# The first three loads of a streaming GELU-multiply kernel: from a critical section into the first block

## Chip, cores, metric

One core of a Trainium2 chip. The metric is the device time of one execution in microseconds (us). A profiled execution also has a span, from its first instruction to its last; the time is some 1.4 us longer than the span.

## The reference

```python
def setup_inputs():
    return {'x': np.random.randn(32, 512, 2048).astype(np.float32)}

def reference(x):
    half_dim = x.shape[-1] // 2
    x1, x2 = x[..., :half_dim].copy(), x[..., half_dim:].copy()
    gelu_x1 = 0.5 * x1 * (1 + erf(x1 / np.sqrt(2)))
    return (gelu_x1 * x2).astype(np.float32)
```

It reads 134.2 MB and writes 67.1 MB.

## The kernel before

The rows are cut into 16 tiles of 128 partitions x 8 rows. There are two input and two output buffers. SyncE issues the loads, ScalarE the GELU and most stores, VectorE the multiply, and the kernel owns all semaphores in the loop. A tile framework wraps only the beginning: it starts with an opening barrier and ends with a closing barrier (made by `tc.close()`), in each of which all engines wait for one another, and the first three loads are issued between the two. A semaphore is a counter that one instruction or transfer raises and another waits for; a load has landed when its semaphore says so.

```python
    def load(i, rows, sem):
        counted(
            nc.sync.dma_start(out=x_bufs[i % 2][:, rows, :], in_=x_t[i][:, rows, :]), sem, 16
        )
    ...
    with tc.tile_critical():
        load(0, slice(0, 4), first)
        load(0, slice(4, 8), loaded[0])
        load(1, slice(0, 8), loaded[1])
    tc.close()
    tc.compile()

    for i in range(n_tiles):
        k = i % 2
        last = i == n_tiles - 1
        pieces = i == 0 or last
        steps = ((0, 2), (2, 4), (4, 8)) if pieces else ((0, 5), (5, 8))
        if i >= 2:
            nc.scalar.wait_ge(stored[k], n[stored[k].name])
        for lo, hi in steps:
            rows = slice(lo, hi)
            if i == 0 and lo == 0:
                nc.scalar.wait_ge(first, n[first.name])
            elif lo == 0 or (i == 0 and lo == 4):
                nc.scalar.wait_ge(loaded[k], n[loaded[k].name])
            ...  # ScalarE: GELU of these rows; VectorE: multiply; in tile 0 a store, issued by ScalarE, behind rows 4 and 8
        ...      # other tiles: one store
        if i + 2 < n_tiles:
            nc.sync.wait_ge(mul_done, n[mul_done.name])
            load(i + 2, slice(0, R), loaded[k])
```

Of the kernel before, what the change touches and what calls it, by code (L numbers as in the profile page):

```python
# [1 line left out]

# [4 lines left out]

GELU = mybir.ActivationFunctionType.Gelu


@with_exitstack
def kernel(
    ctx: ExitStack,
    tc: tile.TileContext,
    x: bass.AP,
    out: bass.AP,
):
    nc = tc.nc
    P = nc.NUM_PARTITIONS

    x_flat = x.flatten_outer_dims()
    out_flat = out.flatten_outer_dims()
    n_rows, dim = x_flat.shape
    half = dim // 2

    R = 8
    x_t = x_flat.rearrange("(n p r) d -> n p r d", p=P, r=R)
    o_t = out_flat.rearrange("(n p r) d -> n p r d", p=P, r=R)
    n_tiles = x_t.shape[0]
    x_bufs = [nc.alloc_sbuf_tensor(f"x{k}_tile", [P, R, dim], x.dtype) for k in range(2)]  # L30
    o_bufs = [nc.alloc_sbuf_tensor(f"o{k}_tile", [P, R, half], out.dtype) for k in range(2)]

    first = nc.alloc_semaphore("first")
    loaded = [nc.alloc_semaphore(f"loaded{k}") for k in range(2)]
    stored = [nc.alloc_semaphore(f"stored{k}") for k in range(2)]
    gelu_done = nc.alloc_semaphore("gelu_done")
    mul_done = nc.alloc_semaphore("mul_done")
    tail_stored = nc.alloc_semaphore("tail_stored")
    n = {sem.name: 0 for sem in [first, *loaded, *stored, gelu_done, mul_done, tail_stored]}

    def counted(ins, sem, by):
        ins.then_inc(sem, by)
        n[sem.name] += by

    def load(i, rows, sem):
        counted(
            nc.sync.dma_start(out=x_bufs[i % 2][:, rows, :], in_=x_t[i][:, rows, :]), sem, 16  # L47
        )

    def store(queue, i, rows, sem):  # L50
        queue.wait_ge(mul_done, n[mul_done.name])
        counted(
            queue.dma_start(out=o_t[i][:, rows, :], in_=o_bufs[i % 2][:, rows, :]), sem, 16
        )



    with tc.tile_critical():  # L58
        load(0, slice(0, 4), first)
        load(0, slice(4, 8), loaded[0])  # L60
        load(1, slice(0, 8), loaded[1])
    tc.close()
    tc.compile()  # L63

# [14 lines that stand above are left out]
                nc.scalar.activation(  # L79
                    out=o_bufs[k][:, rows, :], in_=x_bufs[k][:, rows, :half], func=GELU  # L80
                ),
                gelu_done,
                1,
            )
            nc.vector.wait_ge(gelu_done, n[gelu_done.name])
            counted(
                nc.vector.tensor_mul(  # L87
                    out=o_bufs[k][:, rows, :],
                    in0=o_bufs[k][:, rows, :],
                    in1=x_bufs[k][:, rows, half:],  # L90
                ),
                mul_done,
                1,
            )
            if pieces and hi % 4 == 0:
                if last:
                    store(nc.sync, i, slice(hi - 4, hi), tail_stored)
                else:
                    store(nc.scalar, i, slice(hi - 4, hi), stored[k])
        if not pieces:  # L100
            if i == n_tiles - 2:
                store(nc.sync, i, slice(0, R), tail_stored)
            else:
                store(nc.scalar, i, slice(0, R), stored[k])
# [5 lines that stand above are left out]
    nc.scalar.drain()  # L110
    for sem in (first, *loaded, *stored):
        nc.scalar.sem_clear(sem)
    nc.vector.drain()
    nc.vector.sem_clear(gelu_done)
    nc.sync.sem_clear(mul_done)
    nc.sync.wait_ge(tail_stored, n[tail_stored.name]).then_inc(
        tail_stored, -n[tail_stored.name]
    )


# [1 line left out]
_INS = ['x']  # L122
_OUTS = [((32, 512, 1024), 'float32')]


# [23 lines left out]
```

## Time and profile before

| | before |
|---|---|
| time, median of the first 3 runs | 469.57 us (469.43 to 469.67) |
| span of the profiled run | 468.1 us |
| VectorE / ScalarE busy | 30% / 25% |
| DMA, mean over the span | 430 GB/s |
| first load issued / first packet / first activation | 0.94 / 1.95 / 12.99 us |

Read it from the ends inward. The compute engines are mostly idle and the DMA engines are busy throughout, so what counts is when the stream of 201.3 MB starts, whether it has holes, and its rate. The prediction shows the lines for each.

### The profile page before, as it was taken

What the parts mean: (1) busy time and instruction counts of PE and PEld (TensorE: products, weight loads), DVE (VectorE), ACT (ScalarE), POOL (GpSimd) and SP (SyncE); (2) the same over time, 40 slices, a digit from 0 to 9 for tenths busy, and PEclk for the clock granted to TensorE, in tenths of its full rate; (3) what the DMA queues carried; (4) which work ended last, traced back from release to release, by engine and by line L of the source; (5) the groups of instructions that cost most, each with busy time, mean ns of one, the idle gap of its engine ahead of it and who ended that gap; (6) DMA issues with size and microseconds to landing.
All of it is one profiled execution on the core that took longest, in us unless ns stands there. A gap on an engine that the chain in (4) does not pass through costs nothing.

```text
span 468.1 us, 174 instructions
## 1 busy us (share of the span) xinstructions
DVE 140.5 (30%) x34; ACT 115.5 (25%) x35; POOL 0.2 (0%) x4
## 2 busy tenths in 40 slices
DVE  0330514207052060511606116060150702507043
ACT  1320606032060410604106050050500506014060
POOL 0000000000000000000000000000000000000000
DMA  8999899999999999999999999999999999999998
GB/s 358 448 448 442 375 423 496 414 403 445 417 482 403 420 431 493 403 403 448 470 426 403 442 409 493 403 403 448 493 403 403 448 442 454 404 428 423 493 395 367
DMA packets 5041, 201.34 MB, mean 430 GB/s; under 512 B 560, under 2 KB 560, under 8 KB 560
## 3 DMA queue, kind: packets, MB, share of 16 engines
q1 hardware_dynamic: 2880, 142.61, 70.5%
q10 hardware_dynamic: 2160, 58.72, 29.1%
q14 instruction: 1, 0.01, 0.0%
HBM read 134.22 MB, written 67.11 MB: 430 GB/s over the span
## 4 chain that ended last, share of the span: by engine, by line
DMA 76%; DVE 14%; ACT 8%; ACTq 0%; SPq 0%; issue 0%
DMA out_dram<-o_tile 66%; DVE o_tile L87 14%; DMA x_tile<-in_x_dram 10%; ACT o_tile L79 8%; ACTq L110 0%; SPq L47 0%; SPq L63 0%; SPq L58 0%
## 5 line engine op out<-in xcount | busy, mean ns | idle before, releaser
L87 DVE TENSOR_TENSOR o_tile<-o_tile,x_tile 128x5120 f32<-128x5120 f32 (+3 forms) x34 | 140.5, 4170 | 320.2 <-ACT o_tile L79 320.2
L79 ACT ACTIVATE o_tile<-x_tile 128x5120 f32<-128x5120 f32 (+3 forms) x34 | 114.3, 3407 | 337.4 <-DMA out_dram<-o_tile 301.9
L79 ACT ACT_TABLE_LOAD x1 | 1.3, 1283 | 3.3 <-PEq L63 3.3
L133 POOL MEMSET const-bfloat16-1.0<- 128x1 bf16 x1 | 0.1, 102 | 0.0
L133 POOL MEMSET const-uint8-127<- 128x1 uint8 x1 | 0.1, 102 | 0.0
L133 POOL MEMSET const-float32-1.0<- 128x1 f32 x1 | 0.1, 99 | 0.0
L133 POOL MEMSET const-float32-0.0<- 128x1 f32 x1 | 0.1, 98 | 0.2 <-issue 0.2
## 6 DMA issues: line engine op xcount, KB each, us to landing
out_dram<-o_tile ACTq DMA_DIRECT2D x13, 4096.0 KB, 44.7
x_tile<-in_x_dram SPq DMA_DIRECT2D x2, 4096.0 KB, 16.7
out_dram<-o_tile ACTq DMA_DIRECT2D x2, 2048.0 KB, 34.4
out_dram<-o_tile SPq DMA_DIRECT2D x1, 4096.0 KB, 25.1
out_dram<-o_tile SPq DMA_DIRECT2D x2, 2048.0 KB, 7.6
x_tile<-in_x_dram SPq DMA_DIRECT2D x15, 44.5
```

Source lines behind the costliest of these rows:

```text
L79: nc.scalar.activation(out=o_bufs[k][:, rows, :], in_=x_bufs[k][:, rows, :half], func=GELU),
L87: nc.vector.tensor_mul(out=o_bufs[k][:, rows, :], in0=o_bufs[k][:, rows, :], in1=x_bufs[k][:, rows, half:],),
L133: nc = _bacc.Bacc("TRN2", target_bir_lowering=False, num_devices=1)
```

## The change

Intent: the critical section costs SyncE a nop and a branch ahead of the loads and some bookkeeping behind them. The new version issues the same loads as plain instructions of the framework's first block, and marks them so that the framework adds no semaphores of its own. The marking is needed: left out, the kernel does not build, as the framework then finds no room on these instructions for its own semaphore update.

```diff
     def load(i, rows, sem):
-        counted(
-            nc.sync.dma_start(out=x_bufs[i % 2][:, rows, :], in_=x_t[i][:, rows, :]), sem, 16
-        )
+        ins = nc.sync.dma_start(out=x_bufs[i % 2][:, rows, :], in_=x_t[i][:, rows, :])
+        counted(ins, sem, 16)
+        return ins
...
-    with tc.tile_critical():
-        load(0, slice(0, 4), first)
-        load(0, slice(4, 8), loaded[0])
-        load(1, slice(0, 8), loaded[1])
+    for ins in (
+        load(0, slice(0, 4), first),
+        load(0, slice(4, 8), loaded[0]),
+        load(1, slice(0, 8), loaded[1]),
+    ):
+        tc.no_tile_sem_insts.add(ins.ins.name)
     tc.close()
     tc.compile()
```

## The prediction

> **What bounds the kernel now.** I read the page first (spans, the 40 slices, the chain, the DMA queues), then the stretches table for the stages, then the chain in order of time, then the instructions of source lines L58, L47 and L63, because the change touches only the first 3.3 us.
>
> ```profile
> span 468.1 us, 174 instructions
> DVE 140.5 (30%) x34; ACT 115.5 (25%) x35; POOL 0.2 (0%) x4
> DMA  8999899999999999999999999999999999999998
> HBM read 134.22 MB, written 67.11 MB: 430 GB/s over the span
> ```
>
> Neither compute engine is busy a third of the span, while the DMA engines are in the top tenth in nearly every slice, the first and the last included. The stretches table gives the same by stage (columns: stretch, its length, busy time and instructions of VectorE, ScalarE and GpSimd, clock, DMA share, GB/s):
>
> ```profile
> 0.00:40.00 40.00, 8.92 (x3) 8.61 (x4) 0.20 (x4) 1.00 0.96 406
> ...
> 118.00:176.00 58.00, 17.52 (x4) 14.24 (x4) 0.00 (x0) 1.00 1.00 434
> ...
> 292.00:350.00 58.00, 17.52 (x4) 14.25 (x4) 0.00 (x0) 1.00 1.00 434
> ```
>
> The steady rate is 434 GB/s and two tiles (25.2 MB) take 58.0 us. The chain of waits puts 76% of the span on DMA; its other pieces (9 us of VectorE, 4.5 us of ScalarE) are latency while the DMA engines work on other tiles, as the full share of these stretches shows. So the kernel is a stream of 201.3 MB. A change can help only by starting the stream earlier, speeding it, or filling a hole in it. Before the stream there is this head of the chain:
>
> ```profile
> 0.67 0.05 issue
> 0.71 0.01 SPq L58
> 0.73 0.06 issue
> 0.78 0.03 SPq L63
> 0.82 0.12 issue
> 0.94 0.38 SPq L47
> ```
>
> L58 is the critical section, L47 the load. SyncE leaves the opening barrier at 0.67 us, runs a NOP of the critical section at 0.71, a compare-and-branch at 0.78 that leads into its block, and issues the first load only at 0.94. Finer stretches show when bytes move:
>
> ```profile
> 1.84:1.95 0.11, 0.00 (x0) 0.00 (x0) 0.00 (x0) 1.00 0.00 0
> 1.95:2.05 0.10, 0.00 (x0) 0.00 (x0) 0.00 (x0) 1.00 6.70 1966
> ...
> 466.00:467.00 1.00, 0.00 (x0) 0.00 (x0) 0.00 (x0) 1.00 0.99 426
> 467.00:468.00 1.00, 0.00 (x0) 0.00 (x0) 0.00 (x0) 1.00 0.05 16
> ```
>
> The first packets start at 1.95 us, 1.0 us after the first load's issue begins; the last end just after 467.0, and the final wait passes at 468.1. (A share over 1 appears because packets are booked at their start.) Hence: 0.94 us of prologue, 1.0 us of first latency, about 465.1 us of stream, 1.0 us of last latency. The reported 469.57 us is 1.4 us more than the span, a constant that I carry over.
>
> After the loads, the critical section and the closing of the block stand between SyncE and the barrier that frees the others:
>
> ```profile
> L58 SPq NOP  x2: 13/13/13, 0.7 to 2.5; - x2
> L58 SPq EVENT_SEMAPHORE  x1: 17/17/17, 2.3 to 2.3; - x1
> L58 SPq DRAIN  x1: 55/55/55, 2.4 to 2.4; - x1
> ```
>
> ScalarE waits behind that barrier until 3.28 us, loads its table for 1.28 us, and then waits again for the first load, which lands at 12.97:
>
> ```profile
> 3.28 1.28 ACT L79 ACT_TABLE_LOAD   x1 [3.28 <-PEq L63]
> 12.99 3.71 ACT L79 ACTIVATE o_tile<-x_tile 128x2048 f32<-128x2048 f32 x2 [8.43 <-DMA x_tile<-in_x_dram]
> ```
>
> It has 8.43 us of slack there.
>
> **What the Trainium skill says.** "DMA: Bandwidth & Descriptors", section "Where 436 GB/s comes from", gives 435.2 GB/s for the 16 ports; the trace agrees with 434 in the steady stretches, so the stream has nothing left to gain from a different start. The same page, "Latency and other measured facts", gives about 600 ns for the first byte of a hardware-generated DMA; the trace differs with 1.0 us from issue start to first packet, and I use 1.0. "Advanced Engine Details and Errata", "Control Flow Timing", gives about 108 ns for a compare-and-branch; the trace has 0.03 us recorded plus 0.12 us before the next instruction starts, 0.15 in all. "ScalarE: Activation LUTs", "What ACT_TABLE_LOAD costs", gives about 1283 ns; the trace agrees with 1.28 us.
>
> **The change part by part.** (1) *Removed ahead of the loads:* the entry NOP (0.71) and the branch with the gap behind it (to 0.94). If the loads stand in the first block, the first takes the NOP's place right after the opening barrier. 0.94 - 0.71 = 0.23 us, all on the path: the stream starts 0.23 us sooner, the first packets at about 1.72. (2) *Unchanged:* the three loads, their order, queue, sizes and semaphores. Their issue costs 0.94 to 2.27 = 1.33 us in total, and becomes 0.71 to about 2.04. Marking them as owned by the kernel only keeps the framework from adding its own semaphores and waits. (3) *Removed behind the loads:* the exit's semaphore event, drain and NOP, from 2.27 to 2.57 on SyncE, 0.3 us less perhaps 0.05 for the ordinary step to the next instruction, so about 0.25. With part 1 the closing barrier frees ScalarE about 0.23 + 0.25 = 0.48 us sooner, at about 2.8 instead of 3.28. That lies inside the 8.43 us of slack and is worth nothing. (4) *Moved:* the first activation waits for the first load, so it moves from 12.99 to about 12.76; from there each tile's work hangs on landings and on stores, and these shift by the same 0.23 us. Nothing in the loop changes, so no hole is filled and the rate stays 434 GB/s. Sum: -0.23 us on the path, +0; span 468.1 to about 467.9, time 469.57 to 469.34.
>
> **The rivals.** *A: the gain is swallowed.* The branch might stay ahead of the loads, or the first packets might wait on something that does not depend on the issue. For it: the first packets come 1.0 us after issue, longer than the page's 0.6. Against it: the branch carries a wait on the critical section's own semaphore and goes only to SyncE, so it belongs to the section. Time: 469.6. *B: the closing barrier now waits for the loads.* A section that hides its DMAs is gone, and a framework that waits at the block's end for every DMA in flight would hold ScalarE until all three loads land. They are 16.8 MB, at 434 GB/s some 38.7 us, so to about 40.5. Then come the barrier's rest (2.64 to 3.28, 0.64), the table (1.28), and ScalarE and VectorE from the first activation to the first store's issue (12.99 to 19.45, 6.46): the DMA engines would idle some 8.4 us plus the latency to the first byte, 1.0. Time: 469.3 + 9.4 = about 479, +2.0%. Against it: the point of marking the instructions is to leave them out of that bookkeeping. I give it 2 to 3%. *C: the framework's scheduler reorders the three loads*, for example the 8-row load ahead of tile 0's second half. The first store at 19.45 would stay; the second half would land only with the whole 16.8 MB plus the first store's 2.1 MB, near 45 us, and tile 0's reuse load and second store (issued at 30.80 now) would come only some 8 us of compute later (3.62 + 4.43), so again a hole of at most 8 us: about 477. Against it: all three are on one engine with no dependence among them; source order is the natural one. About 1%. *D: the new start disturbs the interleaving of loads and stores.* Both streams hang on the same events and move together, and the unchanged runs spread only 0.24 us; I allow 0.3 us either way.
>
> **Range and chances.** The centre is the main sum, rounded: 469.3. Rival A is 0.3 above; run-to-run spread is 0.24 us, and another chip or session can add a few tenths; 0.15% is 0.7 us. So 468.7 to 469.9. A gain of 2% (9.4 us) would need a hole in the stream that no stretch shows, or a rate above the 434 at which it already runs: 0.5%. A loss of over 2% needs B at the large end of its estimate: 1.5%. Within 2%: 98%.
>
> **What would show it right or wrong.** In the changed profile: no L58-like NOP or compare-and-branch ahead of the first load; its issue begins at 0.70 to 0.75; first packets at 1.7 to 1.75; the three issues still sum to about 1.33; the table load begins near 2.8; the first activation at about 12.76; loads and stores 0.2 us sooner everywhere; stretches of 58 us at 434 GB/s. Step 1 is wrong if the first issue stays near 0.94 (rival A) or if the first packets do not follow it. Rival B would show as a table load near 41 us, rival C as a second half of tile 0 landing after 40 us with the first activation still near 12.8, D as a later shift different from that of the first activation. My step 4 fails if the shift at the start is there, but the end comes no sooner.

## The result, and the profile after

| | before | after |
|---|---|---|
| time, median of 6 runs each | 469.59 us (469.43 to 469.67) | 469.38 us (469.27 to 469.52) |
| span of the profiled run | 468.1 us | 468.0 us |
| first load issued | 0.94 us | 0.73 us |
| first packet | 1.95 us | 1.74 us |
| table load of ScalarE | 3.28 us | 2.86 us |
| first activation | 12.99 us | 12.79 us |

The ratio is 0.9996, with a 95% interval of 0.9983 to 1.0009. The interval includes 1: these twelve runs alone do not show a gain, the experiments below pool more.

The chain of waits of the kernel after, in order of time (start, length, what), begins without the nop and the branch. SPq is an instruction in SyncE's queue, "issue" is time in which the engine waited for nothing that the profile shows; the load's line is now L46:

```profile
0.67 0.07 issue
0.73 0.38 SPq L46
1.11 0.05 issue
1.17 0.43 SPq L46
1.59 0.05 issue
1.64 45.50 DMA x_tile<-in_x_dram
```

SyncE leaves the opening barrier at 0.67 as before, and its next instruction is the load. Fine stretches of the kernel after (columns as in the prediction, the last is GB/s) show the bytes following by 1.0 us, the same steady rate, and an end that comes a few packets earlier (311 GB/s between 466 and 467 us, where the kernel before still had 426):

```profile
1.64:1.74 0.10, 0.00 (x0) 0.00 (x0) 0.00 (x0) 1.00 0.00 0
1.74:1.84 0.10, 0.00 (x0) 0.00 (x0) 0.00 (x0) 1.00 5.69 1638
118.00:176.00 58.00, 17.52 (x4) 14.24 (x4) 0.00 (x0) 1.00 1.00 434
466.00:467.00 1.00, 0.00 (x0) 0.00 (x0) 0.00 (x0) 1.00 0.73 311
```

The timeline of ScalarE in the kernel after (start, length, instruction, idle time before it and what ended it):

```profile
2.86 1.28 ACT L82 ACT_TABLE_LOAD   x1 [2.86 <-PEq L66]
12.79 3.71 ACT L82 ACTIVATE o_tile<-x_tile 128x2048 f32<-128x2048 f32 x2 [8.64 <-DMA x_tile<-in_x_dram]
```

The table load came 0.42 us earlier, and ScalarE only waits longer for the first load (8.64 us instead of 8.43). The activation moved by 0.20, as the load's issue did.

One thing in this pair of traces needed care: the shift is 0.20 us at the first activation, but 0.14 at the third tile-load's landing (47.28 against 47.14) and 0.11 at the end of the span. Was a part of the gain lost on the way, or is that noise?

### The profile page after: what moved, and what is told of

Same layout as the page of the kernel before. It is cut to its first block, busy times and chain, and to the rows that moved or that the text cites. A ratio compares the mean times of both kernels' runs of the same rounds, so it can differ in the third digit from the quotient of the medians.

```text
span 468.0 us, 167 instructions
## 1 busy us (share of the span) xinstructions
DVE 140.5 (30%) x34; ACT 115.5 (25%) x35; POOL 0.2 (0%) x4
## 4 chain that ended last, share of the span: by engine, by line
DMA 76%; DVE 14%; ACT 8%; ACTq 0%; SPq 0%; issue 0%
DMA out_dram<-o_tile 66%; DVE o_tile L90 14%; DMA x_tile<-in_x_dram 10%; ACT o_tile L82 8%; ACTq L113 0%; SPq L46 0%
```

## Experiments

The theory is that the time is the first load's issue plus a constant, the stream behind it. The main rivals: the earlier closing barrier makes the gain rather than the earlier loads; or the start is hidden and the 0.2 us are noise.

### The two kernels again

The first is the kernel before, unedited, the second the kernel after, unedited; so neither has a diff.

> The kernel before against itself, to learn how small a difference five rounds can show. Every theory: ratio 1.0000, medians within 0.1 us of each other, first load issued at 0.94 us, first activation at 12.99 us give or take 0.05, span 468.0 to 468.2 us. If the two medians differ by 0.2 us or more, the measured gain of the change (469.59 to 469.38) is not distinguishable from noise by times alone.

Measured: 469.56 us median of 5, against 469.54 for the other runs of the kernel before in those rounds; ratio 0.9998. The two means are 469.53 and 469.64, so even equal kernels differ by 0.1 us in one set of rounds: a single set cannot settle 0.2 us. The first load was issued at 0.94 us, the first activation came at 13.02, the span was 468.2.

> The changed kernel unedited, again. Main theory (the whole stream is moved forward by the earlier issue): 0.1 to 0.25 us faster than before, first load issued at 0.73 us, first activation near 12.79. In the first profile the shift against the kernel before was 0.20 us at the first issue and at the first activation but only 0.14 at the third landing and 0.10 at the last packet; if that loss is noise of the memory, this profile shows other values in the late stages with the same 0.20 at the start; if it is systematic, it shows the same decay. Rival A (gain swallowed): no difference in time.

Measured: 469.31 us median of 5 (469.22 to 469.60), ratio 0.9995 (0.9981 to 1.0008). The first load was again issued at 0.73. But the first activation came at 12.90 and the span was 468.2 us. So two profiles of the same kernel, with the same issue time, differ by 0.11 us at the first activation and by 0.2 us at the end. The "decay" of the shift in the first pair of traces is within that, and single profiles cannot resolve 0.2 us at the end of the span; the start of the loads, which repeats to 0.01 us, and many timed runs can. Over all runs the kernel before has a mean of 469.57 us (31 runs) and the kernel after one of 469.39 us (11 runs): 0.18 us, with a standard error that I put at 0.05 from the spread of some 0.13 us of single runs. The issue moved by 0.20 us. The kernel after ran beside the kernel before twice, and each time the means give much the same (0.18 us in the result, 0.21 us here).

### One part of the change at a time

An empty critical section put back behind the loads. The exit is back where it was; in the trace the section's own nop and branch come with it, but also behind the loads (2.10 and 2.17 us):

```diff
         tc.no_tile_sem_insts.add(ins.ins.name)
+    with tc.tile_critical():
+        nc.sync.nop(nofuse=True)
     tc.close()
```

> The changed kernel with an empty critical section behind the three loads: the exit instructions are back, the entry ones stay away from the loads. Main theory: first load issued at 0.73 us, ScalarE's table load starts later than the changed kernel's 2.86, at 3.1 to 3.4, and the time is that of the changed kernel (within 0.1 us), since ScalarE has over 8 us of slack there. Rival (the earlier closing barrier is what gains): the time goes back to that of the kernel before, +0.2 us.

Only the entry left: the kernel before, with the three instructions behind its loads taken out of the built program:

```diff
     tc.compile()
+    behind = next(b for b in nc.main_func.blocks if "_after_critical" in b.name)
+    behind.instructions = [
+        ins for ins in behind.instructions
+        if type(ins).__name__ not in ("InstNoOp", "InstDrain")
+    ]
```

> The kernel before with the three exit instructions of the critical section (nop, drain, nop) taken out; the loads still stand behind its entry nop and branch. Main theory: first load issued at 0.94 us, table load starts some 0.2 us earlier than 3.28, and the time is that of the kernel before (within 0.1 us). Rival (the exit is what cost the time): 0.2 us faster than before.

Measured: exit back, 469.37 us median of 5, first load at 0.73, table load at 3.26. Entry back, 469.45 us median of 5, first load at 0.94, table load at 3.13. The first is clear: a whole critical section behind the loads costs nothing measurable. The second lay between the two kernels, so I ran it again, together with a large dose of the other factor.

> The version with only the entry of the critical section left, again, as its first five runs (mean 469.46 us) lay between the two kernels: 0.07 us above the changed kernel and 0.11 below the kernel before. Main theory: the time of the kernel before, near 469.57 us, so that the mean of the ten runs is within 0.1 us of it. Rival: 469.4 again or less, and then the exit instructions have a share of some 0.1 us in the gain that the main theory does not explain.

Measured: 469.54 us median of 5 (469.53 to 469.60). The mean of the ten runs is 469.51 us, within 0.1 of the kernel before (469.57), as expected, though not so clean that a share of some hundredths of a microsecond could be excluded. (The first five ran on one chip and the second five on another.)

The dose: a VectorE instruction of no use in the first block, which holds the closing barrier.

```diff
         tc.no_tile_sem_insts.add(ins.ins.name)
+    nc.vector.memset(o_bufs[1][:, 0:8, :], 0.0)
     tc.close()
```

> The changed kernel with a VectorE memset of 128x8192 float32, of no other use (6.9 us in the held run), in the first block: the closing barrier waits for VectorE's drain, so ScalarE is freed some 5 us later while the loads are issued as early as ever. Main theory (the closing barrier is off the path): first load at 0.73 us, table load near 8.2 us instead of 2.86, done by 9.5, first activation near 12.8 and the time that of the changed kernel, within 0.1 us. Rival (a later barrier costs time, as the exit instructions were thought to): +5 us, or any growth over 0.2 us.

Measured: 469.47 us median of 6, mean 469.43, against 469.39 for the kernel after. In the timeline of this run:

```profile
0.73 1.33 SPq L46 DMA_DIRECT2D x_tile<-in_x_dram  x3
2.50 6.88 DVE L65 MEMSET o_tile<- 128x8192 f32 x1 [2.50 <-issue]
9.98 1.28 ACT L83 ACT_TABLE_LOAD   x1 [9.98 <-PEq L67]
12.78 1.91 ACT L83 ACTIVATE o_tile<-x_tile 128x2048 f32<-128x2048 f32 x1 [1.52 <-DMA x_tile<-in_x_dram]
```

ScalarE was freed 7.1 us later than in the kernel after (9.98 against 2.86), and the first activation came at 12.78 all the same: the slack shrank from 8.64 to 1.52 us and took all of it. The start of the table load was a miss of mine (8.2 expected): VectorE began the memset only at 2.50 us. So 7.1 us of delay at the closing barrier cost at most some 0.1 us (0.04 by these means, which come from two chips), and the 0.42 us by which the change moves it are worth nothing measurable.

Sorted by the first load's issue alone, the two kernels and their variants agree. In the four profiles with the issue at 0.73 us (after, twice; exit back; slack) the first activation came at 12.78 to 12.90 us, in the four with 0.94 (before, twice; entry back, twice) at 12.99 to 13.06; the means are 0.20 us apart. All their timed runs give 469.40 us (22 runs) and 469.55 us (41 runs), 0.16 us apart with a standard error of some 0.03.

### The start of the stream, in small and large doses

Later: the loads behind the closing barrier.

```diff
-    for ins in (
-        load(0, slice(0, 4), first),
-        ...
-    ):
-        tc.no_tile_sem_insts.add(ins.ins.name)
     tc.close()
     tc.compile()
+    load(0, slice(0, 4), first)
+    load(0, slice(4, 8), loaded[0])
+    load(1, slice(0, 8), loaded[1])
```

> The changed kernel with the three loads behind the closing barrier instead of ahead of it. The first load should then be issued at some 1.4 to 1.7 us (two barriers of about 0.4 us each from 0.7 on) instead of 0.73. Main theory (each microsecond of later issue is one microsecond of time): span = first issue + 467.3 us, so 468.7 to 469.0, and a time 0.7 to 1.0 us longer than the changed kernel's. Rival A (the start is hidden): unchanged time.

Much later: the same, with a wait ahead of the first load (and the semaphore `go` allocated and cleared).

```diff
     tc.compile()
+    nc.vector.memset(o_bufs[1][:, 0:8, :], 0.0).then_inc(go, 1)
+    nc.sync.wait_ge(go, 1)
     load(0, slice(0, 4), first)
```

> As the late version, but SyncE waits ahead of the first load for one VectorE memset of 128x8192 float32, which has no other use; a large dose of the same delay. [...]Main theory: span = first issue + 467.3 us again, so the time grows by just what the first issue does. If some of the delay were absorbed by the stream (a faster restart, holes filled), the growth would be smaller by over 0.5 us.

Earlier: the three instructions moved, in the built program, ahead of SyncE's part in the opening barrier. They read and write nothing that the barrier protects. The outputs are right.

```diff
     tc.compile()
+    main, opening = nc.main_func.blocks[0], nc.main_func.blocks[1]
+    names = [ins.ins.name for ins in early]      # the three loads
+    moved = [ins for ins in opening.instructions if ins.name in names]
+    opening.instructions = [ins for ins in opening.instructions if ins.name not in names]
+    at = next(k for k, ins in enumerate(main.instructions)
+              if type(ins).__name__ == "InstDrain" and str(ins.engine).endswith("SP"))
+    main.instructions = main.instructions[:at] + moved + main.instructions[at:]
```

> The changed kernel with its three loads moved ahead of the opening barrier, to the head of SyncE's instructions, which start at the span's 0. Main theory: first issue near 0.1 us, or before the span's present start; the first packets 1.0 us after it; time shorter than the changed kernel's by about 0.6 us (0.73 minus the new first issue). A rival: the first packets stay near 1.7 us since the DMA engines or the runtime's start set them; then no gain.

And the early version with its first load cut, to see whether the 1.0 us to the first packet is descriptor work:

```diff
-        load(0, slice(0, 4), first),
+        load(0, slice(0, 1), first),
+        load(0, slice(1, 4), first),
```

> The early version (loads ahead of the opening barrier) with its first load cut into one row and three rows. If the first packets wait for the generation of the whole first load's descriptors, they start sooner than 1.0 us after the first issue, and the time falls below the early version's 468.68 us by up to 0.3 us. If the 1.0 us is a fixed latency, the first packets stay at 1.0 us, and the time stays within 0.1 us of the early version's or grows by the added issue.

Measured, with the difference of the first two columns:

| kernel | first load issued | mean time (runs) | time less issue |
|---|---|---|---|
| early | 0.00 us | 468.66 us (5) | 468.66 us |
| after | 0.73 us | 469.39 us (11) | 468.66 us |
| before | 0.94 us | 469.57 us (31) | 468.63 us |
| late | 1.38 us | 469.94 us (5) | 468.56 us |
| held | 10.07 us | 478.74 us (4) | 468.67 us |

Over 10 us of delay the time less the issue stays within 0.11 us: the start is passed on whole, neither hidden nor made up for later. The early, late and held versions ran on another chip than the repeat of the kernel after; on that chip the kernel before had a mean of 469.53 us (11 runs), 468.59 less its issue, so the agreement does not come from mixing chips. The late version's issue came sooner than I had expected (1.38 instead of 1.4 to 1.7), and its time, 0.55 us over that of the kernel after, missed my 0.7 to 1.0 for that reason and by 0.1 us that is within the noise (against the kernel before on the same chip it is 0.41 us of time for 0.44 us of issue). The chain of waits of the held version shows the dose on the path:

```profile
3.16 6.90 DVE o_tile L62
10.06 0.02 issue
10.07 0.38 SPq L47
```

The early version is the fastest: 468.68 us median, ratio to before 0.9981 (0.9969 to 0.9994), an interval that excludes 1. The chain of waits of the early version and its fine stretches:

```profile
0.00 0.37 SPq L46
0.37 0.05 issue
```

```profile
0.90:1.00 0.10, 0.00 (x0) 0.00 (x0) 0.00 (x0) 1.00 0.00 0
1.00:1.10 0.10, 0.00 (x0) 0.00 (x0) 0.00 (x0) 1.00 7.92 2294
```

The packets again come 1.0 us after the issue. With the first load cut into one row and three, they came at 1.02 us, and the time was 468.65 us (median of 6): the 1.0 us does not depend on the first load's size in these two sizes. The first activation came 0.2 us sooner (11.87 instead of 12.10), without effect on the time.

### The rivals of the prediction, made on purpose

Rival B, the closing barrier waiting for the loads:

```diff
         tc.no_tile_sem_insts.add(ins.ins.name)
+    nc.sync.wait_ge(loaded[1], 16)
     tc.close()
```

> The changed kernel with SyncE waiting for the third load ahead of the closing barrier: rival B of the prediction made on purpose. The prediction's estimate: table load near 41 us, time about 479 us (+9.4). If the DMA engines idle for less than I worked out (they have nothing queued until the first store), the time is smaller.

Measured, one run (state unknown, granted clock 1.0): 484.12 us, 14.7 over the kernel after, where the estimate was 9.4. Stretches and timeline of this run:

```profile
40.00:42.00 2.00, 0.00 (x0) 0.00 (x0) 0.00 (x0) 1.00 0.00 0
...
48.00:50.00 2.00, 2.00 (x2) 0.00 (x0) 0.00 (x0) 1.00 0.00 0
...
56.00:58.00 2.00, 2.00 (x1) 0.00 (x0) 0.00 (x0) 1.00 0.00 0
```

```profile
42.58 1.28 ACT L83 ACT_TABLE_LOAD   x1 [42.58 <-PEq L67]
...
50.34 0.38 ACTq L53 DMA_DIRECT2D out_dram<-o_tile  x1
50.76 3.62 ACT L83 ACTIVATE o_tile<-x_tile 128x4096 f32<-128x4096 f32 x1 [3.18 <-DVE o_tile L91]
...
58.87 0.36 ACTq L53 DMA_DIRECT2D out_dram<-o_tile  x1
```

The last column of the stretches, which books a packet at its start, has two holes, one from 40 us and one around 57, where I had foreseen one. By the trace's packet records, which have ends too, no packet was under way from 41.4 to 51.2 us (9.9 us) and from 56.3 to 59.8 (3.5 us), 13.4 of the 14.7 us. The first hole is close to the 9.4 foreseen. The table load was at 42.58 instead of 41, as the third load landed at 41.8 us and not at the estimated 40.5. The second hole I had missed. ScalarE issues tile 0's first store (50.34) and waits for VectorE ahead of it; its queue is in order, so the third activation stands behind that wait (3.18 us idle, released by VectorE) although its data had long been there. The next store and the next load come only at 58.87.

Rival C, the order of the loads:

```diff
-        load(0, slice(4, 8), loaded[0]),
-        load(1, slice(0, 8), loaded[1]),
+        load(1, slice(0, 8), loaded[1]),
+        load(0, slice(4, 8), loaded[0]),
```

> The changed kernel with the 8-row load of tile 1 ahead of the second half of tile 0: rival C of the prediction made on purpose. The prediction's estimate: first activation still near 12.8 us, the second half of tile 0 lands near 45 us, and the time is about 477 us. By what the held-barrier run showed (ScalarE's queue is in order, so tile 1's first activation stands behind tile 0's last store), tile 1, though loaded early, cannot be worked on either until tile 0 is done; a hole of some 8 us then, which may well be 1 or 2 us larger.

Measured, one run (state unknown, granted clock 1.0): 480.89 us, 11.5 over the kernel after; the estimate in the prediction was about 477. The first activation came at 12.76 as foreseen, and the second half of tile 0 landed at 47.5 (not 45). This run's timeline:

```profile
55.61 0.36 ACTq L53 DMA_DIRECT2D out_dram<-o_tile  x1
56.02 7.12 ACT L82 ACTIVATE o_tile<-x_tile 128x5120 f32<-128x5120 f32 x2 [4.90 <-DVE o_tile L90]
```

Tile 1's first activation stood behind tile 0's last store, idle 4.90 us on VectorE: the same in-order wait. But the packet records have one hole only, from 47.1 to 56.6 us: 9.4 us, as this run's expectation had allowed, where the prediction had at most 8. The other 2.1 of the 11.5 us were not traced. Neither rival occurred in the changed kernel; the two runs price what they would have cost.

## Why the prediction was right

- *The bound.* Right: the rate in the steady stretches is 434 GB/s before and after, and the time follows the start of the stream one to one over 10 us.
- *Step 1, the entry on the path, -0.23 us.* Right in mechanism, and nearly in size: the issue moved from 0.94 to 0.73, by 0.20 (0.204 unrounded) and not 0.23, as the load starts at 0.73 where the nop had stood at 0.71. The first packets moved by the same. The timed runs give 0.18 with a standard error of 0.05.
- *Step 2, the loads themselves unchanged.* Right: 0.73 to 2.06, 1.33 us in all, in the same order.
- *Step 3, the exit worth nothing, table load at 2.8.* Right: 2.86 (0.42 sooner instead of 0.48), and a barrier 7.1 us later cost nothing measurable. What the exit had done did not vanish whole: the closing block's first SyncE drain took 123 ns behind the loads, where it had been 7 ns behind the critical section's own drain of 55 ns.
- *Step 4, the shift kept to the end.* Right, but not provable from the two traces that the prediction named as the test: their ends differ by 0.11 us, and two profiles of the same kernel differ by 0.2 us there.
- *Rival A* is excluded by the doses. What the prediction counted for it, a first packet later than the page's 0.6 us, comes from counting from the beginning of the issue (see the last section). *Rival D* cannot be told from noise: later stages shift by 0.1 to 0.2 us between two profiles of the same kernel, and of the 0.20 us some 0.16 to 0.18 arrive in the time, with standard errors of 0.03 and 0.05.
- *Rivals B and C* did not occur, but I had priced them too low: 484.1 and 480.9 us instead of 479 and 477. For B the failed step is that the hole was taken for one, ended by the first store: that one was priced nearly right (9.4 against 9.9 us), but ScalarE's in-order queue adds a second of 3.5 us. For C it is the size of a single hole, 9.4 instead of 8 us: the estimate counted the compute time (8.1 us here) and left out the 1.0 us from the store's issue to its first packet and 0.4 us from the last packet to the activation. The remaining 1.3 us of B and 2.1 us of C stay open. Both were over 2% slower (3.1% and 2.4%, in one run each), so the chance of "slower" should have been their full chance, 3 to 4%, not 1.5%.
- *Time.* 469.3 said, 469.38 measured, inside 468.7 to 469.9. The few tenths allowed for another chip or session were not needed: the means of the kernel before in the three groups of runs (the result, r1, r2 to r4) are 469.57, 469.60 and 469.53 us.

## What to carry to other kernels

In this kernel, one long DMA stream, the instructions ahead of the first load were on the path one to one, and those behind it were free as long as the consumers had slack (8.4 us here). In a kernel of this kind, look first at the head of the issuing engine's queue, and try to move the first loads ahead of everything that they don't depend on, the opening barrier included (0.7 us here). Price such a change before making it: the ceiling was 0.94 us of 469.6. A difference of 0.2 us is read from the issue times and from many runs, not from where one profile ends; and when you price a delay, follow the in-order queue of the engine that also issues stores.

## What the Trainium skill lacked or had wrong

- "DMA: Bandwidth & Descriptors", "Latency and other measured facts": gives about 600 ns for a hardware-generated DMA's first byte, but not from when it counts. Here the first packet started 1.00 to 1.03 us after the issue instruction began, and 0.62 to 0.65 us after it ended, in every profile, with a first load of one row as of four. Counted from the end, the figure agrees; the prediction's "the trace differs" holds only for the beginning.
- "Advanced Engine Details and Errata", "Control Flow Timing": about 108 ns for a compare-and-branch, without saying between which points. Here the record was 33 ns long, and the next instruction began 153 ns after its start; the nop and the branch together put the load off by 0.20 us.
- No page that I found has it: SyncE's drain took 7 ns in most places, but 123 to 127 ns as the next instruction behind the three loads (123 in the kernel after, 127 with the entry back, 125 in the early version).
- No page that I found has it: VectorE's first compute instruction, a memset, started 1.8 us after the barrier that freed it (1.38 to 3.16 us in the held version, and at 2.50 us in the run with the memset in the first block). The cause was not looked into.
